# Two feed-forward projections by seven block products each instead of eight

## The chip, the cores and the metric

The kernel runs on one core of a Trainium2 chip: TensorE (PE in the rows, PEld its weight loads), VectorE (DVE), ScalarE (ACT), GpSimd (POOL), and SyncE (SP), whose queue issues nearly all DMA transfers. The metric is the device time of one execution in microseconds (us), the median of several runs.

## The reference, cut to what matters

One layer of a decoder works on 1032 tokens, 1024 of a prompt and 8 of a sample, with 1024 channels in float32:

```python
def layer_forward(h, p_i, ...):
    u = rmsnorm(h, lw['norm_mix'])
    proj = u @ lw['w_in']
    ...
    h = h + jnp.concatenate([y_a, y_b, y_c], axis=-1) @ lw['w_out']
    z = jnp.square(jax.nn.relu(rmsnorm(h, lw['norm_ffn']) @ lw['w_up']))
    h = h + z @ lw['w_down']
    gate = jax.nn.sigmoid(rmsnorm(h, lw['norm_ple']) @ lw['w_ple_gate'])
    h = h + gate * (p_i @ lw['w_ple_proj'])
```

`w_up` is 1024 by 4096, `w_down` 4096 by 1024, the gate's weights 1024 by 1024, and the embedding's projection 256 by 1024. A final norm over `h` gives the output.

## The kernel before, in words

Channels lie on the 128 partitions, tokens along the free axis: a tile is [128, 1032]. The residual `h` is eight such tiles, which stay in SBUF from the output projection to the end. A product keeps float32 accuracy by splitting both operands into a high and a low part of the fast matmul type: three matmuls (weight high times activation high, high times low, low times high; L256, L257, L258) stand for one. A product of 1032 tokens is made as three chunks of 344 columns, each in a PSUM bank of its own.

Weights come in blocks of 512 KB ([128, 1024]). A ring of three raw tiles takes them (L196, SP's queue); ACT writes the high part (L205), DVE or POOL the low part, raw minus high (L206). The ring for high and low parts has three places too.

The stages are: the input projection and, beside it, the three mixers; the output projection, which adds into `h`; the feed-forward; the gate with the embedding; the final norm. The feed-forward goes in eight blocks of 512 hidden channels. Per block four weight blocks go up (8 contraction tiles x 3 x 3 chunks = 72 matmuls each) and four go down (72 each): 64 x 72 = 4608 matmuls. The next block's first up product is put before a block's down products. The eviction of an up chunk is `evac_up`: DVE rectifies and scales by the norm's factor (L1155), ACT squares (L1156), DVE writes the high part (L1157) and the low part (L1158) into tiles which the down products read at once. The eviction of a down chunk is one addition into `h` from PSUM (L1092). POOL has nothing to do here.

In the gate stage the 1024 by 1024 gate product runs over two spans of 384 tokens first, for all eight output tiles, and then over the last 264 tokens. Per output tile the embedding's product (12 matmuls a tile in the first pass, 6 in the second) follows it in a second bank, and `evac_gate` takes both banks. The final norm's factor is turned and spread over the partitions by small matmuls (L307) which stand amid the 264-wide part; POOL multiplies 768 columns a tile by it (L1269), and the last 264 are finished at the end (L1282 to L1293).

The order on each engine is not written by hand: the program's builder orders instructions by a list schedule with costs and priorities of its own, and each engine works its list in that order. Transfers are issued on eight lanes, so that a ninth waits for the oldest of the eight.

Of the kernel before, what the change touches and what calls it, by code (L numbers as in the profile page):

```python
# [8 lines left out]
F32 = mybir.dt.float32  # L9
# [13 lines left out]
LEVELS = (1, 2, 4, 8, 16, 32, 64)  # L23

VEC = {}          # name -> (first column, columns) in the table of per-channel vectors
# [8 lines left out]
TAB = {}          # name -> (first column, columns) in the table of constants  # L34
# [18 lines left out]
class Builder:  # L53
# [7 lines left out]
    def pools(self):  # L61
# [5 lines left out]
        pp = ctx.enter_context(tc.tile_pool(name="psum", bufs=1, space=bass.MemoryType.PSUM))  # L67
# [9 lines left out]
        self.bank = [pp.tile([128, 512], F32, name=f"ps{i}") for i in range(8)]  # L77
        self.mains, self.P = deque(self.bank[:4]), deque(self.bank[4:])

# [50 lines left out]
    def step(self):  # L130
        """One stage of the next chain that can go on; False if none can."""
# [52 lines left out]
    def weights(self, aps):  # L184
        """The blocks to come, each with the engine for its low part."""
# [4 lines left out]
    def entry(self, i):  # L190
        """Block i's tiles: high part, low part, raw."""
# [38 lines left out]
    def tile_mm_k(self, i, kof, xs, evac, free=None):  # L230
        """As tile_mm with the K tiles outside, for operands that come or go one by one."""
# [43 lines left out]
    def rsqrt(self, out, v, t):  # L275
        """out = v ** -0.5: a guess from the exponent, a Newton step of tuned constants (to 7e-4), a cubic step."""
# [1154 lines left out]
```

## Time and profile before

The time is 1633.91 us, the median of 3 runs (1630.21 to 1635.50). The profiled execution has a span of 1635.9 us.

| | PE | DVE | ACT | POOL |
|---|---|---|---|---|
| busy, us | 1586.9 | 978.9 | 436.6 | 285.6 |
| share of the span | 97% | 60% | 27% | 17% |
| instructions | 10251 | 1761 | 558 | 267 |

A row of groups reads: line, engine, operation, output and inputs by their names in the program, shapes and types, count, then busy time in us, mean in ns, and idle time of the engine just before with what ended it. A row of a window lists the stretch, then for PE, PE's weight load, DVE, ACT and POOL the busy time and the number of instructions, then the clock that TensorE was granted (1.00 is full), the share of the DMA engines and GB/s. A row of a timeline begins with the start and the duration in us.

### The profile page before, as it was taken

The page shows a single profiled execution, that of the slowest core. Times are in us where ns is not written, and L with a number is a line of the kernel's source. Part 1 is how long each engine was busy: PE and PEld are TensorE (multiplying, and loading weights), DVE is VectorE, ACT ScalarE, POOL GpSimd, SP SyncE. Part 2 cuts the span into 40 slices and gives each one's busy share as a digit, 9 for nine tenths or more (in the row PEclk, how much of TensorE's full clock was granted, in tenths as well). Part 3 has the DMA queues.
Part 4 walks back from the last instruction along what each step waited for, and adds up shares of the span by engine and source line. Part 5 has one row for each costly group of instructions (what it writes and reads, how often), then busy time and mean ns, then how long its engine had stood idle before and what let it go on. Part 6 is the DMA issues. An engine that isn't in the chain of part 4 may idle for free.

```text
span 1635.9 us, 24167 instructions
## 1 busy us (share of the span) xinstructions
PE 1586.9 (97%) x10251; PEld 1561.6 (95%) x10251; DVE 978.9 (60%) x1761; ACT 436.6 (27%) x558; POOL 285.6 (17%) x267
## 2 busy tenths in 40 slices
PE   7999999999989898999999999999999999999995
PEld 7999999998989898999999999999999999999995
DVE  7787877975887977456534444343444434466556
ACT  5212111124464372133211111120211111134442
POOL 5333233224255442000000000000000000012204
PEclk9999999999999998999999999999999999999998
DMA  5011111111211234241111111111111111121123
GB/s 205 28 34 47 44 47 34 40 53 59 67 54 52 94 119 139 91 146 49 39 52 51 41 52 39 52 49 42 52 39 52 52 40 52 39 78 65 52 65 117
DMA packets 34364, 103.21 MB, mean 63 GB/s; under 512 B 5584, under 2 KB 8272, under 8 KB 34256
## 3 DMA queue, kind: packets, MB, share of 16 engines
q1 hardware_dynamic: 34256, 101.67, 19.4%
q8 instruction: 80, 1.31, 0.3%
q14 instruction: 28, 0.23, 0.0%
HBM read 87.39 MB, written 14.26 MB: 62 GB/s over the span
## 4 chain that ended last, share of the span: by engine, by line
PE 70%; DVE 10%; ACT 2%; issue 2%; POOL 2%; DMA 1%; SPq 0%; POOLq 0%; ACTq 0%; DVEq 0%
PE ps L257 21%; PE ps L256 21%; PE ps L258 21%; DVE g L336 2%; PE ps L414 1%; POOL f L1269 1%; PE ps L240 1%; DVE g L420 1%; PE ps L746 1%; DVE g L334 1%; PE ps L852 1%; DMA o_sss<-f 1%; DVE g L866 0%; DVE f L816 0%; PE ps L307 0%
## 5 line engine op out<-in xcount | busy, mean ns | idle before, releaser
L257 PE MATMUL ps<-r,wh 128*128 128x344 f32 (+2 forms) x2700 | 877.8, 325 | 0.0
L256 PE MATMUL ps<-r,wh 128*128 128x344 f32 (+2 forms) x2700 | 875.4, 324 | 0.0
L258 PE MATMUL ps<-r,wl 128*128 128x344 f32 (+2 forms) x2700 | 871.5, 323 | 0.0
L257 PEld LDWEIGHTS ps<-r,wh 128*128 128x128 f32 x2700 | 510.1, 189 | 3.5 <-issue 2.2
L256 PEld LDWEIGHTS ps<-r,wh 128*128 128x128 f32 x2700 | 510.6, 189 | 2.7 <-issue 1.7
L258 PEld LDWEIGHTS ps<-r,wl 128*128 128x128 f32 x2700 | 510.2, 189 | 3.1 <-issue 1.7
L205 ACT ACTIVATE wh<-raw 128x1024 fp32r<-128x1024 f32 x123 | 130.3, 1059 | 625.4 <-PE ps L257 461.4
L1092 DVE TENSOR_TENSOR f<-f,ps 128x344 f32<-128x344 f32 x240 | 122.2, 511 | 232.4 <-PE ps L258 229.1
L329 POOL TENSOR_TENSOR r<-f,r 128x1032 fp32r<-128x1032 f32 x2 | 4.8, 2408 | 790.8 <-ACT r L328 790.8
L1155 DVE SCALAR_TENSOR_TENSOR f<-ps,f 128x344 f32<-128x344 f32 x96 | 49.5, 516 | 139.2 <-PE ps L258 137.7
L206 POOL TENSOR_TENSOR wl<-raw,wh 128x1024 fp32r<-128x1024 f32 x39 | 96.4, 2473 | 197.2 <-ACT wh L205 197.0
L206 DVE TENSOR_TENSOR wl<-raw,wh 128x1024 fp32r<-128x1024 f32 x84 | 105.8, 1260 | 35.0 <-ACT wh L205 34.7
L1156 ACT ACTIVATE f<-f 128x344 f32<-128x344 f32 x96 | 46.6, 486 | 188.8 <-DVE f L1155 188.7
L1157 DVE CAST r<-f 128x344 fp32r<-128x344 f32 x96 | 36.3, 378 | 34.8 <-ACT f L1156 34.7
L1158 DVE TENSOR_TENSOR r<-f,r 128x344 fp32r<-128x344 f32 x96 | 49.5, 517 | 2.9
L420 DVE COPY_PREDICATED g<-tab,ps 128x512 f32<-128x512 int32 x42 | 37.3, 892 | 14.8 <-PE ps L414 14.2
L414 PE MATMUL ps<-f,g 128*128 128x128 f32 x336 | 45.0, 278 | 0.8 <-DVE g L430 0.8
L414 PEld LDWEIGHTS ps<-f,g 128*128 128x128 f32 x336 | 42.6, 191 | 1.9 <-DVE g L430 1.7
L1005 DVE TENSOR_TENSOR g<-ps,f 128x344 f32<-128x344 f32 x63 | 32.0, 509 | 12.8 <-PE ps L258 9.4
L323 ACT ACTIVATE r<-f,vec 128x1032 fp32r<-128x1032 f32 (+1 forms) x26 | 28.1, 1085 | 35.5 <-DVE f L1092 33.0
L324 DVE SCALAR_TENSOR_TENSOR r<-f,vec,r 128x1032 fp32r<-128x1032 f32 (+1 forms) x26 | 33.7, 1298 | 4.3 <-ACT r L323 4.1
L683 POOL TENSOR_TENSOR r<-tab,dtl 128x256 fp32r<-128x256 f32 x32 | 25.9, 813 | 57.7 <-PE ps L736 56.5
(428 smaller groups left out, 1625.8 us busy)
## 6 DMA issues: line engine op xcount, KB each, us to landing
raw<-wu SPq DMA_DIRECT2D x32, 512.0 KB, 3.6
raw<-wd SPq DMA_DIRECT2D x32, 512.0 KB, 3.5
raw<-win SPq DMA_DIRECT2D x31, 512.0 KB, 3.6
raw<-wg SPq DMA_DIRECT2D x16, 512.0 KB, 3.6
f<-x SPq DMA_DIRECT2D x15, 516.0 KB, 5.7
raw<-wo SPq DMA_DIRECT2D x12, 512.0 KB, 3.7
o_y<-f SPq DMA_DIRECT2D x8, 384.0 KB, 2.3
g<-ya SPq DMA_DIRECT2D x4, 516.0 KB, 4.7
```

Source lines behind the costliest of these rows:

```text
L205: self.nc.scalar.activation(wh, raw, AF.Copy)
L206: self.wq[i][1].tensor_tensor(wl, raw, wh.bitcast(F32), op=OP.subtract)
L256: nc.tensor.matmul(ps, a, xh[:, cs], start=(k == 0), stop=False)
L257: nc.tensor.matmul(ps, a, xl[:, cs], start=False, stop=False)
L258: nc.tensor.matmul(ps, b, xh[:, cs], start=False, stop=(k == last))
L414: nc.tensor.matmul(ps[:, w * 128:(w + 1) * 128].rearrange("p (h k m) -> p h k m", h=2, m=m), d["k"][:, w * 128:(w + 1) * 128], qv[:, :, w ...
L420: V.copy_predicated(d["att"][:, :1024].rearrange("p (a k two m) -> p a k two m", a=8, two=2, m=m)[:, :, :, 1, :], mask.rearrange("p (k m) ...
L1092: V.tensor_tensor(h[m][:, cs], h[m][:, cs], ps, op=OP.add)
L1155: V.scalar_tensor_tensor(tz[:, cs], ps, 0.0, norm.rB[:, cs], op0=OP.max, op1=OP.mult)
L1156: A.activation(tz[:, cs], tz[:, cs], AF.Square)
L1157: V.tensor_copy(hi[:, cs], tz[:, cs])
L1158: V.tensor_tensor(lo[:, cs], tz[:, cs], hi[:, cs].bitcast(F32), op=OP.subtract)
```

## The change

Both feed-forward products are cut into halves of output channels, of contraction and of tokens (516 each), and made by the Winograd form of Strassen's scheme: seven products of half size instead of eight, for which sums of quarters are needed on both sides and sums of products behind.

*Weights.* They are laid out by quarters; four quarter sums per unit are made on POOL (L1529 to L1532), and seven pieces are split into high and low (L347 on ACT, L348 on DVE). This is done by `Feed`, which also issues the transfers (L1525).

*Activations going in.* `PairNorm` replaces the norm that came before the feed-forward: as each output tile of `h` is done, it is scaled (ACT), squared (ACT), summed (POOL or DVE), and stored to DRAM; for each pair of tiles four sums of 516 columns are made (POOL; DVE for the last pair), and seven results are split into high and low. 28 tiles hold these operands.

*Up.* A unit is 256 hidden channels; 16 units of 7 products, each 4 contraction tiles x 3 x 2 chunks of 258 columns = 24 matmuls: 2688. Two chunks lie in two banks, a pair; four pairs take the seven products in the order 0, 2, 1, 0, 2, 1, 3, where products 3, 4 and 5 go on adding to the pair of 0, 1 and 2 (product 3 adds to product 0, 4 to 1, 5 to 2). So each of these three waits until the pair it goes on with has been read out: product 3 for L1262, product 4 for L1264, product 5 for L1266. The four quarters of the hidden activations are squared, and four more are made from them by POOL (L1273 to L1287), one of which is overwritten on the way. The seven operands for the down product are split (L1243 on ACT, L1244 on DVE) into a staging tile, high and low side by side, and stored to DRAM (L1245). Units 14 and 15 stay in SBUF.

*Down.* 32 units: eight blocks of contraction (512 channels, two up units) by four pairs of output tiles, each unit 7 products of 12 matmuls: 2688. `h` is loaded again from DRAM (L1372), the products are read out by DVE and ACT, and sums of results on POOL finish three of the four quarters. The operands of a block are loaded again while the block before is at work: 14 tiles of 516 KB at its end (L1418), the first 14 in the first unit (L1415).

*Embedding.* Its product (192 matmuls of 258 columns) now stands between up and down; its result goes to DRAM (L1359) and is loaded again for the gate stage (L1167), where `evac_gate` reads it from SBUF instead of from PSUM. The gate stage has the gate product alone.

PSUM is cut anew twice, into four pairs for the feed-forward and back into eight banks. In the changed program L275 to L277 are the three matmuls of `mm_chunk`, L316 and L326 the two small products of the final norm, and L224/L225 the weights' high and low parts outside the feed-forward.

```diff
-        norm = self.trunk_norm(h, "norm_ffn")
+        norm = PairNorm(self, h, "norm_ffn")
+        up = Feed(self, [io["wu"][i] for i in range(16)], 512, [self.raw[k] for k in (2, 0, 1)],
+                  [self.wr[k] for k in (2, 0, 1)])
...
-        for i, (kind, b, m) in enumerate(order):
-            if kind == "u":
-                self.tile_mm(i, 0, hg, evac_up(b, m))
...
-                    self.tile_mm(i, n * 4, z4, add_h(mm, norm2.add if b == 7 else None), ahead=(n == 0))
...
+        norm.rest()
+        up.advance(0)
+        self.pair = self.psum("pp", 4)
+        zd = self.ffn_up(norm, up)
+        h = self.ffn_down(norm, up, zd)
...
-                for s, ps, pe in zip(spans, pg, pp):
-                    self.mm_chunk(pe, *wp[m // 4], (m % 4) * 2, p, s)
-                    evac_gate(m, s, ps, pe)
+                for s, ps in zip(spans, pg):
+                    evac_gate(m, s, ps, pe[m][:, s])
...
+    def product(self, n, w, q, ks, last):
+        wh, wl, off = w
+        acc = self.pair[ACC[n]]
+        for k in ks:
+            a, b = (t[:, off + k * 128:off + (k + 1) * 128] for t in (wh, wl))
+            for i, (l, o) in enumerate(((a, 0), (a, HF), (b, 0))):
+                for c in range(2):
+                    self.nc.tensor.matmul(acc[:, c * 512:c * 512 + CQ], l, q[k][n][:, o + c * CQ:o + (c + 1) * CQ],
...
+        def spill(n, t):
...
+            A.activation(hi.bitcast(F32R), t, AF.Copy)
+            V.tensor_tensor(lo.bitcast(F32R), t, hi, op=OP.subtract)
+            nc.sync.dma_start(zd[-1][n], st)
...
+        def act(t, r, src=None):
+            V.scalar_tensor_tensor(two(t), two(t) if src is None else src, 0.0, two(r), op0=OP.max, op1=OP.mult)
+            A.activation(t, t, AF.Square)
+
+        def evac(n):
+            ps = self.acc(n)
+            if n == 0:
+                A.activation(two(t1), ps, AF.Copy)
+            elif n == 1:
+                A.activation(two(t5), ps, AF.Copy)
+            elif n == 2:
+                V.tensor_tensor(two(t2), ps, two(t1), op=OP.subtract)
+            elif n == 3:
+                act(a0, rb[0], ps)
+                spill(0, a0)
+            elif n == 4:
+                V.tensor_tensor(two(a1), ps, two(t2), op=OP.subtract)
+                act(a1, rb[1])
+                G.tensor_tensor(v1, a0, a1, op=OP.subtract)
+                spill(1, v1)
+            elif n == 5:
+                V.tensor_tensor(two(t3), ps, two(t1), op=OP.subtract)
+                G.tensor_tensor(b1, t3, t5, op=OP.subtract)
+                act(b1, rb[1])
+                G.tensor_tensor(t2_, b1, v1, op=OP.add)
+                spill(4, b1)
+                G.tensor_tensor(v3, a1, b1, op=OP.subtract)
+                spill(2, t2_)
+                spill(5, v3)
+            else:
+                V.tensor_tensor(two(b0), ps, two(t3), op=OP.add)
+                act(b0, rb[0])
+                G.tensor_tensor(v4, b0, t2_, op=OP.subtract)
+                spill(3, b0)
+                spill(6, v4)
...
+                    if j == 3 and b < 6:
+                        for k in range(2):
+                            nc.sync.dma_start(qs[k][n].bitcast(F32), zd[2 * b + 2 + k][n])
...
+                if i == self.groups - 1:
+                    a11, s1, s2, a12, s4, a21, a22 = (self.piece(u, n) for n in range(7))
+                    G.tensor_tensor(s1, a21, a22, op=OP.add)
+                    G.tensor_tensor(s2, s1, a11, op=OP.add)
+                    G.tensor_tensor(s4, s2, a12, op=OP.add)
+                    G.tensor_tensor(a21, a21, a11, op=OP.add)
```

In a row of the order stands the line, the operation, output and inputs by tile (`f` a float32 tile, `r` a tile of split operands, `wh` and `wl` weights' high and low parts, `raw` weights as loaded, `ps` and `pp` PSUM banks and pairs) and the shape. In the kernel before, DVE in the middle of an up product of the feed-forward works through these rows:

```order
L1155 SCALAR_TENSOR_TENSOR f4_96<-ps3_111,f8_100 128x344 [waits PE_49]
L206 TENSOR_TENSOR wl0_87<-raw0_90,wh0_86 128x1024 [waits DMAHW2_49,Activation_49]
L1157 CAST r2_6_5572<-f4_96 128x344 [waits Activation_49]
L1158 TENSOR_TENSOR r2_7_5573<-f4_96,r2_6_5572 128x344 [waits DVE_49]
L1155 SCALAR_TENSOR_TENSOR f7_99<-ps0_108,f8_100 128x344 [waits PE_49]
```

In the change, DVE in a steady up unit, around the reads of products 2 (L1266), 3 (L1256 from `pp0`) and 4 (L1271):

```order
L1244 TENSOR_TENSOR f1_90<-f8_97,f1_90 128x516 [waits DMAHW6_49,Activation_49]
L1244 TENSOR_TENSOR f4_93<-f3_92,f4_93 128x516 [waits DMAHW0_49,Activation_49]
L1266 TENSOR_TENSOR f0_89<-pp1_6209,f0_89 128x516 [waits PE_49]
L1244 TENSOR_TENSOR f11_100<-f8_97,f11_100 128x516 [waits DMAHW2_49,Activation_49]
L1256 SCALAR_TENSOR_TENSOR f5_94<-pp0_6208,f6_95 128x516 [waits PE_49]
L348 TENSOR_TENSOR wl2_5564<-raw1_88,wh2_5563 128x1024 [waits Activation_49]
L1244 TENSOR_TENSOR f1_90<-f5_94,f1_90 128x516 [waits DMAHW3_49,DVE_49,Activation_49]
L1271 TENSOR_TENSOR f5_94<-pp2_6210,f0_89 128x516 [waits PE_49]
L1256 SCALAR_TENSOR_TENSOR f5_94<-f5_94,f6_95 128x516 [waits DVE_49]
L1276 TENSOR_TENSOR f2_91<-pp1_6209,f0_89 128x516 [waits PE_49]
```

Where evictions stood with one low part of a weight among them, low parts of the unit before (L1244), which wait for ACT and for the store that last used their staging tile (the DMAHW semaphores), now stand before and between the reads of PSUM. POOL, which had no row in the feed-forward, has nine in each up unit of the change:

```order
L1273 TENSOR_TENSOR f10_99<-f5_94 128x516 [waits Activation_49]
L1277 TENSOR_TENSOR f3_92<-f2_91 128x516 [waits DVE_49]
L1279 TENSOR_TENSOR f10_99<-f3_92,f10_99 128x516 [waits Activation_49]
L1281 TENSOR_TENSOR f8_97<-f5_94,f3_92 128x516
L1529 TENSOR_TENSOR raw0_87<-raw2_5565,f7_96 128x512 [waits DMAHW2_49,DMAHW0_49]
L1287 TENSOR_TENSOR f8_97<-f3_92,f10_99 128x516 [waits Activation_49,Pool_49]
L1530 TENSOR_TENSOR raw1_88<-raw0_87 128x512 [waits DMAHW1_49,Pool_49]
L1532 TENSOR_TENSOR raw2_5565<-raw2_5565,raw0_87 128x512
L1531 TENSOR_TENSOR raw2_5565<-raw1_88 128x512 [waits DMAHW6_49,Pool_49]
```

All nine have two operands in SBUF (a name that stands once covers two halves of one tile), and the sums of weights stand among those of results. SP at the end of a down block, where SP before had a weight block now and then:

```order
L1525 DMA raw1_88<-wd 128x256 [waits DMAHW6_49]
L1418 DMA r2_8_5574<-z4_0_7166 128x1032 [waits DMAHW7_49,PE_49]
L1418 DMA r3_69<-z5_0_7397 128x1032 [waits DMAHW0_49,PE_49]
L1418 DMA r2_9_5575<-z4_1_7167 128x1032 [waits DMAHW1_49,PE_49]
L1418 DMA r4_70<-z5_1_7398 128x1032 [waits DMAHW2_49,PE_49]
...
L1418 DMA r0_66<-z4_4_7170 128x1032 [waits DMAHW7_49,PE_49]
L1525 DMA raw0_87<-wd 128x256 [waits DMAHW0_49,DVE_49]
L1525 DMA raw0_87<-wd 128x256 [waits DMAHW1_49,Pool_49]
L1418 DMA r7_73<-z5_4_7401 128x1032 [waits DMAHW2_49,PE_49]
L1525 DMA raw1_88<-wd 128x256 [waits DMAHW3_49,DVE_49]
L1418 DMA r1_67<-z4_5_7171 128x1032 [waits DMAHW4_49,PE_49]
```

The reloads wait for PE to be done with the tiles of the block before (PE_49), and pieces of weights (L1525) stand behind them in the one queue.

More of the change, by code (lines that the diff above doesn't have):

```diff
@@ L1209, in build @@
                 wh, wl = self.block(i)
-                pg, pp = ([self.main_bank()[:, :s.stop - s.start] for s in spans] for _ in range(2))
+                pg = [self.main_bank()[:, :s.stop - s.start] for s in spans]
                 for s, ps in zip(spans, pg):
@@ new lines, in embed_part, with embed @@
+    def embed_part(self, n, raw, hi, lo):
+        w = T if n < 2 else 1024
+        self.nc.sync.dma_start(raw[:, :w], self.io["p" if n < 2 else "wp"][n % 2])
+        self.split(raw[:, :w], hi[:, :w], lo[:, :w])
+    def embed(self, q, out):
+        self.pe, nc = [], self.nc
+        for m in range(8):
+            t = out[m % 2]
+            d = self.dp.tile([128, T], F32, name=f"pe{m}")
+            for s in range(2):
+                acc = self.pair[(0, 2, 1, 3)[(2 * m + s) % 4]]
+                for k in range(2):
+                    xh, xl = q[0][k], q[1][k]
+                    wh, wl = (q[i][2 + m // 4][:, (m % 4 * 2 + k) * 128:(m % 4 * 2 + k + 1) * 128] for i in (0, 1))
+                    for i, (l, r) in enumerate(((wh, xh), (wh, xl), (wl, xh))):
+                        for c in range(2):
+                            o = s * HF + c * CQ
+                            nc.tensor.matmul(acc[:, c * 512:c * 512 + CQ], l, r[:, o:o + CQ],
+                                             start=(k == 0 and i == 0), stop=(k == 1 and i == 2))
+                nc.scalar.activation(t[:, s * HF:(s + 1) * HF].rearrange("p (c t) -> p c t", c=2),
+                                     acc.rearrange("p (c t) -> p c t", c=2)[:, :, :CQ], AF.Copy)
+            nc.sync.dma_start(d, t)
+            self.pe.append(d)
@@ new lines, with __init__, add, pair @@
+class PairNorm:
+    def __init__(self, b, h, gname):
+        self.b, self.h, self.gname = b, h, gname
+        self.u, self.q, self.hd, self.later = [], [], [], []
+        self.ssq = self.rB = None
+    def add(self, m):
+        b, nc = self.b, self.b.nc
+        A, G, V = nc.scalar, nc.gpsimd, nc.vector
+        hm = self.h[m]
+        u = b.get_main()
+        A.activation(u, hm, AF.Copy, scale=b.col(self.gname, m))
+        self.u.append(u)
+        if m == 0:
+            self.ssq = b.get_main()
+            A.activation(self.ssq, hm, AF.Square)
+        else:
+            t = b.get_main()
+            A.activation(t, hm, AF.Square)
+            (G if m < 6 else V).tensor_tensor(self.ssq, self.ssq, t, op=OP.add)
+            b.put(t)
+        self.hd.append(b.dp.tile([128, T], F32, name=f"h{m}"))
+        nc.sync.dma_start(self.hd[m], hm)
+        b.put(hm)
+        if m % 2:
+            self.pair(m // 2)
+    def pair(self, k):
+        b, nc = self.b, self.b.nc
+        E = nc.vector if k == 3 else nc.gpsimd
+        ua, ub = self.u[2 * k:2 * k + 2]
+        v = b.get_main()
+        b11, b12, b21, b22, v1, t2 = (t[:, o:o + HF] for t in (ua, ub, v) for o in (0, HF))
+        v3 = b12
+        self.q.append([None] * 7)
+        def split(n, t):
+            def go():
+                q = self.q[k][n] = b.R.popleft()
+                b.split(t, q[:, :HF], q[:, HF:])
+            if b.R and not self.later:
+                go()
+            else:
+                self.later.append(go)
+        split(0, b11)
+        E.tensor_tensor(v1, b11, b12, op=OP.subtract)
+        split(1, v1)
+        E.tensor_tensor(t2, b22, v1, op=OP.add)
+        split(2, t2)
+        split(3, b21)
+        split(4, b22)
+        E.tensor_tensor(v3, b12, b22, op=OP.subtract)
+        split(5, v3)
+        def last():
+            E.tensor_tensor(b21, b21, t2, op=OP.subtract)
+            split(6, b21)
+        if self.later:
+            self.later.append(last)
+        else:
+            last()
+        self.later.append(lambda: b.put(ua, ub, v)) if self.later else b.put(ua, ub, v)
+    def rest(self):
+        todo, self.later = self.later, []
+        for f in todo:
+            f()
+        assert not self.later
+        self.rB = self.b.get_main()
```

253 lines of the change are left out of this document (196 added, 57 removed).

## The prediction

> **What bounds the kernel now.** I read first the totals, the slices and the shares of the chain on the profile's page, then the windows of the feed-forward, then single rows for prices.
>
> ```profile
> span 1635.9 us, 24167 instructions
> PE 1586.9 (97%) x10251; PEld 1561.6 (95%) x10251; DVE 978.9 (60%) x1761; ACT 436.6 (27%) x558; POOL 285.6 (17%) x267
> DVE  7787877975887977456534444343444434466556
> POOL 5333233224255442000000000000000000012204
> PE 70%; DVE 10%; ACT 2%; issue 2%; POOL 2%; DMA 1%; SPq 0%; POOLq 0%; ACTq 0%; DVEq 0%
> ```
>
> PE is busy for 97% of the span and carries 70% of the chain. From slice 17 (about 700 us) to slice 37, DVE is about 40% busy and POOL idle: that is the feed-forward. There every matmul counts, and DVE, ACT, POOL and the DMA queues are covered. The windows give the pace (columns: busy time and instructions of PE, weight load, DVE, ACT, POOL; then clock, DMA share, GB/s):
>
> ```profile
> 0.00:50.00 50.00, 40.05 (x227) 37.22 (x228) 35.56 (x66) 25.03 (x32) 23.10 (x22) 0.97 0.53 179
> 1000.00:1100.00 100.00, 100.00 (x636) 100.00 (x636) 41.24 (x76) 15.64 (x23) 0.00 (x0) 1.00 0.16 48
> 1561.00:1576.00 15.00, 15.00 (x87) 15.00 (x87) 8.79 (x15) 5.74 (x9) 0.00 (x0) 1.00 0.16 47
> 1591.60:1596.60 5.00, 5.00 (x42) 5.00 (x43) 3.97 (x15) 2.26 (x4) 0.00 (x0) 1.00 0.39 102
> ```
>
> 100 us hold 636 matmuls of 344 columns: 157.2 ns each. The third row is the gate stage with 384 columns: 15/87 = 172 to 175 ns. The fourth has 264 columns: 5.00/42 = 119 ns. The time goes with the columns, down to 264. The feed-forward's 4608 matmuls (64 weight blocks of 72) take 4608 x 157.2 = **724.5 us** of the span.
>
> **The change: matmuls.** 48 units (16 up of 7 x 24, 32 down of 7 x 12) issue 5376 matmuls of 258 columns. Of that width there is no row. Bounds: the 264 row less 6 columns at its own slope gives 116, its first starts at most 122; I take 119 ns. An up unit is then 168 x 0.119 = 20.0 us, a down unit 10.0 us, each half 320 us, together 640: 85 us less, where PE never waits. The question is whether the other engines keep that pace, since each unit brings much new work for them.
>
> **The change: an up unit.** Prices, DVE and ACT first, then POOL, then the rows where the two meet (in timeline rows: start, duration; in the others, count, busy, mean ns, or minimum/median/maximum):
>
> ```profile
> L818 DVE TENSOR_TENSOR f<-f 128x512 f32<-128x512 f32 x8 | 5.5, 686 | 1.4 <-POOL f L815 1.3
> L694 DVE TENSOR_TENSOR g<-ps,dt 128x512 f32<-128x512 f32 x6 | 4.0, 685 | 1.2 <-PE ps L692 1.0
> L763 DVE SCALAR_TENSOR_TENSOR g<-g,vec,ps 128x512 f32<-128x512 f32 x8 | 5.9, 740 | 1.2 <-PE ps L761 1.2
> L441 ACT ACTIVATE g<-ps 128x512 f32<-128x512 f32 x5 | 3.0, 598 | 29.0 <-PE ps L440 29.0
> L206 DVE TENSOR_TENSOR wl<-raw,wh x84: 1211/1226/2852, 589.8 to 1609.0; 128x1024 fp32r<-128x1024 f32 x84
> L1269 POOL TENSOR_TENSOR f<-f,f x8: 1845/2044/2825, 1600.2 to 1615.5; 128x768 f32<-128x768 f32 x8
> L1289 POOL TENSOR_TENSOR raw<-f,f 128x264 f32<-128x264 f32 x3 | 2.1, 740 | 11.8 <-ACT f L1282 11.8
> L329 POOL TENSOR_TENSOR r<-f,r 128x1032 fp32r<-128x1032 f32 x2 | 4.8, 2408 | 790.8 <-ACT r L328 790.8
> L205 ACT ACTIVATE wh<-raw 128x1024 fp32r<-128x1024 f32 x123 | 130.3, 1059 | 625.4 <-PE ps L257 461.4
> ```
>
> POOL: 768 columns take 1.845 us and 264 take 0.74, so 2.19 ns a column, and 512 or 516 take 1.28 us. A unit has nine (five of L1273 to L1287, four weight sums of L1529 to L1532): 11.5 us. DVE, two operands in SBUF: 7 low parts of 516 (L1244, 0.69 each), 3 rectifications (L1256, about 0.7), the weights' low parts (L348, three of 1024 at 1.23, one of 512 at 0.69): 14 operations, 11.3 us. DVE, one operand in PSUM: 5 (L1266, L1256, L1271, L1276, L1285) at 0.69: 3.5 us. ACT has 7 high parts, 4 squares, 2 copies and the weights' high parts (1.06 for 1024 columns, 3.8 in all): 13 x 0.62 + 3.8 = 12 us. So DVE 14.8, ACT 12, POOL 11.5 of PE's 20.0: apart, all fit. But before the change POOL stood still in this stage; the end of the program shows DVE beside a busy POOL:
>
> ```profile
> 1600.15 6.63 POOL L1269 TENSOR_TENSOR f<-f,f 128x768 f32<-128x768 f32 x3 [45.68 <-ACT f L318]
> 1598.82 0.43 DVE L1198 TENSOR_TENSOR f<-f,f 128x264 f32<-128x264 f32 x1
> 1600.42 1.87 DVE L1203 TENSOR_TENSOR f<-f,f 128x264 f32<-128x264 f32 x1 [1.17 <-ACT f L1202]
> 1602.21 0.42 DVE L1195 TENSOR_TENSOR f<-ps,f 128x264 f32<-128x264 f32 x1
> 1602.56 2.53 DVE L206 TENSOR_TENSOR wl<-raw,wh 128x1024 fp32r<-128x1024 f32 x1
> 1605.01 0.42 DVE L1197 TENSOR_TENSOR f<-f,ps 128x264 f32<-128x264 f32 x1
> 1605.46 1.62 DVE L1198 TENSOR_TENSOR f<-f,f 128x264 f32<-128x264 f32 x1
> ```
>
> A DVE operation with both operands in SBUF takes 0.43 us alone and 1.62 to 1.87 while POOL works; one that reads PSUM takes 0.42 either way. POOL is stretched too: 1.845 to 2.04 (median) beside a 0.43 us operation, to 2.83 beside one of 1.23 us. So they take turns, and a turn costs POOL 0.20 or 0.98, DVE's own duration less about 0.24; at 516 columns about 0.46. A turn of nine is then 1.28 + 0.46 = 1.74, and nine of them, 15.7 us, let nine of DVE's 14 through (9 x 0.69 = 6.2 of its 11.3 us). The other 5.1 us and the five PSUM reads (3.2 us at a pitch of 0.63) come on top: 24.0, less two PSUM reads which fall under a POOL turn: **22.8 us a unit**, and not 20.0. DVE sets the pace, and PE waits: L1266, which empties product 2's bank for product 5, stands behind low parts of the unit before. Four units are lighter (0 starts without spills in its way, 14 and 15 store nothing): 21 each. Up: 12 x 22.8 + 4 x 21 = **358 us**.
>
> In sentences of their own: the Trainium skill, "SBUF — State Buffer", "Who interferes with whom", says that VectorE and GpSimd share one port pair as an exclusive lock, that a VectorE instruction with two SBUF inputs contends with one of GpSimd that reads SBUF, and that the later fully blocks. The rows agree on who is hit (0.43 against 1.62 to 1.87; 0.42 with PSUM), but not on the whole duration: POOL's row grew by 0.20 for an operation of 0.43.
>
> Stores: 98 tiles of 516 KB go out and come back. With 1 MB of weights an up unit moves 4.6 MB in 22.8 us, 203 GB/s; the first window moved 179 GB/s at a share of 0.53, so the engines of the DMA queues hold it. Three staging tiles rotate, a store has about 9 us until its tile is wanted. I cost the stores at nothing; their cover is that slack.
>
> **A down unit.** POOL 4 sums of 256 (0.72 by the slope) and 3 of 516: 6.7 us. DVE: 6 reads of PSUM (3.8) and the weights' low parts (1.23, and 0.92 for 768 columns): 6.0 us. Should every POOL sum make DVE wait in full for a turn it would be 12.7, but only the two low parts, of 13 operations on the two engines, have both operands in SBUF: with a wait of 1.28 before each, 8.5 of 10.0. PE stays the bound: 320 us. SP now carries the reloads too; at the end of each of six blocks 14 tiles are asked for at once, in front of and between weight pieces (L1525):
>
> ```profile
> raw<-wd SPq DMA_DIRECT2D x32, 512.0 KB, 3.5
> raw_e<-win SPq DMA_DIRECT2D x1, 512.0 KB, 9.9
> ```
>
> Alone 512 KB land in 3.5 us, in the crowd of the first loads in 9.9; weights are fetched about two units (20 us) early. So mostly covered; for seven bursts I add 5 us (bounds 0 and 45, below): **325 us**.
>
> **The way in and the gate.** As the last output tiles come, POOL gets 5 sums of 1032 (2.4 each) and 12 of 516, and the first weights' 4: 32 us, where PE has some 45 us of products; 28 splits on DVE run against it, the last eight after tiles come free. I add **5 us** (0 to 12). The embedding's 192 matmuls before the down half cost 192 x 0.119 = 22.8 us. The gate stage loses 96 of 384 columns (16.8 us) and 48 of 264. The latter gains nothing, because the end hangs on the final factor:
>
> ```profile
> 1584.46 0.29 PE L256 MATMUL ps<-r,wh 128*128 128x264 f32 x1
> 1597.89 1.50 PE L307 MATMUL ps<-ident,nscr 128*128 128x128 f32 x12
> PE ps L307 <- DVE nscr L287: 1.8, 1, 1.8
> ```
>
> L307 comes 13.4 us after the 264 part's start, POOL's L1269 2.3 us later, and 35.8 us after that all is over. In the new order 137 such matmuls precede it instead of 99: 38 x 0.119 = 4.5 us later, less up to 1.8 which PE then waited. Net 22.8 - 16.8 + 3.9 = **9.9 us** (0 to 15).
>
> **Sum** against the profiled 1635.9: 1635.9 - 724.5 + 5 + 358 + 325 + 9.9 = 1609.3. The profiled execution lies 0.1% above the median of the runs, 1633.9; so 1607.
>
> **Rivals.** (1) *No price for turns*: the queues slide past each other, up runs at PE's 20.0: 320 instead of 358, 1607 - 38 = 1569. For it: DVE has 14.8 us of work, and its low parts have a whole unit's slack; against it, the 1.62 to 1.87 rows. (2) *DVE and POOL exclude each other wholly*: 11.5 + 11.3 = 22.8 for the two-operand work, and all five PSUM reads behind it, 3.5: 26.3 us a unit, 16 x 3.5 = 56 more: 1663, slower. The deciding point is 1607 + 16 x (u - 22.8) = 1634: u = 24.5 us a unit. For it: the 2.53 and 2.85 us rows of 1024 columns; against it, POOL's stretch of only 0.20. By the sentence of the Trainium skill on blocking ("SBUF — State Buffer", as above) this would be the outcome. (3) *Reload bursts starve the down half*: the program lets eight transfers be outstanding; 14 tiles at 9.9 us for eight take 17 us, and the weight piece behind it lands up to 6.4 us late, seven times: +45, 1652; slower from 3.9 us a burst on. For it: the order below L1418's rows; against it, the pieces asked for two units early. (4) *The change does less than it says*: it doesn't; the new order holds 2688 + 2688 + 192 matmuls of 258.
>
> **Chances.** The forecast (DVE sets the pace in up, PE in down) 0.57, no price 0.20, full exclusion 0.14, bursts 0.09. The forecast's own range is 1588 to 1630: 116 to 122 ns in the down half gives 8 us either way, the unit's turns 21.5 to 24, the way in 0 to 12, the gate 0 to 15. 8 of 10 takes in most of the no-price case and leaves out the far half of the slow ones: 1566 to 1648. What a measurement can tell from no change is about 0.3%, 1629 to 1639. Faster: 0.20 and nearly all of 0.57: 0.75. Same: the forecast's upper edge, 0.06. Slower: 0.14 + 0.09 less their mild ends, and a little of the forecast: 0.19.
>
> **What would show it.** Right: in windows of the up half PE has about 147 matmuls of 258 columns per 20 us instead of 168, and its waits at the products name DVE's L1266, L1271 and L1276; L1244 means over 1.0 us instead of 0.69, POOL's 516 sums about 1.7. The down half stands at 100% PE, 420 matmuls in 50 us. Wrong: L1244 at 0.7 us and PE full in up (rival 1); units of 25 us and more (rival 2); PE waiting in down for splits of weights whose L1525 pieces landed late (rival 3); a store's tile as the releaser of L1243 would mean the DMA's slack was none; or the first split products waiting more than 12 us at the way in.

## The result

The change makes the kernel slower: 1658.99 us, the median of 4 runs (1657.78 to 1660.30), against 1634.04 us before. The ratio is 1.0156, with a 95% interval of 1.0135 to 1.0176. The forecast was 1607 in a range of 1566 to 1648, so the time lies 11 us outside it and on the other side of the time before.

From the page of the changed kernel (totals, then the busy tenths in slices of 41.5 us each):

```profile
span 1658.2 us, 27796 instructions
PE 1538.6 (93%) x11067; PEld 1504.4 (91%) x11067; DVE 1260.5 (76%) x1798; ACT 607.1 (37%) x810; POOL 825.7 (50%) x650
DVE  7777787876886885559699999989356676679576
POOL 5423232224355441037477666766367677777214
```

PE's busy time fell by 48 us only, DVE's rose by 282 and POOL's by 540. In slices 20 to 27 (the first is 0), the up half, DVE stands at 9, once at 8. The chain of the page can't be set against the 70% of before: here it goes back only to 1099.5 us, and its shares add up to 34% of the span.

The stages can be cut at PE's instructions: start of the second half of the output projection, first and last feed-forward matmul, end. Here are the windows of the kernel before (second half of the output projection, which the table calls the way in, feed-forward, gate and end), and then of the change (the same second half, up, embedding, down, gate and end). The columns are those of the earlier windows.

```profile
720.50:765.70 45.20, 45.20 (x289) 45.20 (x288) 31.52 (x41) 18.71 (x18) 0.00 (x0) 1.00 0.15 48
765.70:1496.60 730.90, 730.90 (x4649) 730.90 (x4648) 323.58 (x567) 132.50 (x183) 9.64 (x4) 1.00 0.16 49
1496.60:1635.90 139.30, 122.85 (x792) 122.45 (x791) 82.71 (x138) 51.95 (x83) 33.91 (x17) 0.94 0.23 76
```

```profile
716.40:778.10 61.70, 47.92 (x290) 46.72 (x288) 49.16 (x52) 32.03 (x42) 39.38 (x21) 0.96 0.26 95
778.10:1148.70 370.60, 343.53 (x2725) 340.62 (x2726) 335.53 (x314) 182.84 (x277) 242.85 (x139) 0.96 0.53 196
1148.70:1184.10 35.40, 26.21 (x193) 24.76 (x193) 17.79 (x18) 14.93 (x27) 16.36 (x13) 0.95 0.86 309
1184.10:1526.20 342.10, 331.16 (x2691) 327.60 (x2690) 230.55 (x261) 92.09 (x110) 245.66 (x212) 0.99 0.55 199
1526.20:1658.20 132.00, 106.24 (x649) 104.44 (x647) 87.28 (x142) 52.91 (x84) 39.82 (x20) 0.88 0.28 98
```

The feed-forward before took 730.9 us, and the forecast takes 724.5 of them out. The 6.4 that it leaves belong to 36 small matmuls of the norm's factor, about 4 us, and to a matmul of 344 columns that takes 157.7 ns from start to start and not 157.2. In the change the 36 stand in the first two up units, so the table puts the 6.4 there.

| stage | forecast, us | measured, us | difference |
|---|---|---|---|
| up to the second half of the output projection | 720.5 | 716.4 | -4.1 |
| way in (45.2 before) | 50.2 | 61.7 | +11.5 |
| up, 16 units (358), with the 6.4 left over | 364.4 | 370.6 | +6.2 |
| embedding | 22.8 | 35.4 | +12.6 |
| down, 32 units | 325 | 342.1 | +17.1 |
| gate and end (139.3 before) | 126.4 | 132.0 | +5.6 |
| sum | 1609.3 | 1658.2 | +48.9 |

No stage missed by more than 17.1 us; five of them missed in the same direction. What PE waited for, the longest and those of the gate's start (engine, line, whom for; us in all, times, longest):

```profile
PE pp L1218 <- DVE f L1266: 24.3, 11, 3.5
PE ps L275 <- DVE f L1111: 7.5, 3, 4.1
PE pp L1355 <- ACT f L1357: 7.4, 5, 3.3
PE pp L1218 <- DVE f L1111: 6.3, 1, 6.3
PE pp L1218 <- ACT wh L347: 5.3, 3, 2.5
PE pp L1218 <- DVE f L1384: 3.3, 1, 3.3
PE pe L275 <- ACT r L342: 3.2, 1, 3.2
PE pe L276 <- DVE r L343: 2.3, 1, 2.3
```

The first row is the forecast's wait in the up half. The second and fourth are the way in, the third the embedding, the next two the down half, and the last two the gate's start.

The waits are not all that PE loses, because its clock falls behind some of them. These are PE's first products of the up half, after a wait of 6.26 us, and a group of four matmuls 5 us later:

```profile
778.06 1.20 PE L1218 MATMUL pp<-r,wh 128*128 128x258 f32 x4 [6.26 <-DVE f L1111]
779.49 1.06 PE L1218 MATMUL pp<-r,wh 128*128 128x258 f32 x4
783.22 0.64 PE L1218 MATMUL pp<-r,wh 128*128 128x258 f32 x4
```

And in the up half, behind a wait of 2.62 us:

```profile
936.87 1.23 PE L1218 MATMUL pp<-r,wh 128*128 128x258 f32 x4 [2.62 <-DVE f L1266]
938.32 1.06 PE L1218 MATMUL pp<-r,wh 128*128 128x258 f32 x4
940.52 0.64 PE L1218 MATMUL pp<-r,wh 128*128 128x258 f32 x4
```

The clock's record shows stretches at half rate, 3.4 us long or a multiple of that. Behind the middle of the program (from 700 us on) they cost 39 us of clock in the change, and 9 before, all of the latter at the very end, where PE has little to do. 9 of the 39 lie there too. In the up half they are 14 us, and the 12 behind its first unit fall on time in which DVE sets the pace (from 828 to 1104 us DVE waits for PE once, 0.5 us). The others, in the way in, at the first up products, in the embedding, the down half and at the gate's start, lie on PE's path, but for some 2 us in which PE waits anyway.

### The profile page after: what moved, and what is told of

The parts are those of the page before. It is cut to its first block, busy times and chain, and to the rows that moved or that the text cites. A ratio compares the mean times of both kernels' runs of the same rounds, so it can differ in the third digit from the quotient of the medians.

```text
span 1658.2 us, 27796 instructions
## 1 busy us (share of the span) xinstructions
PE 1538.6 (93%) x11067; PEld 1504.4 (91%) x11067; DVE 1260.5 (76%) x1798; ACT 607.1 (37%) x810; POOL 825.7 (50%) x650
## 5 line engine op out<-in xcount | busy, mean ns | idle before, releaser
L1218 PE MATMUL pp<-r,wh 128*128 128x258 f32 x3584 | 589.8, 288 | 43.6 <-DVE f L1266 24.3
L1218 PEld LDWEIGHTS pp<-r,wh 128*128 128x128 f32 x3584 | 503.9, 194 | 49.5 <-DVE f L1266 26.9
L1218 PE MATMUL pp<-r,wl 128*128 128x258 f32 x1792 | 362.9, 286 | 0.7 <-DVE wl L348 0.5
L275 PE MATMUL ps<-r,wh 128*128 128x344 f32 x972 | 323.2, 333 | 7.5 <-DVE f L1111 7.5
L276 PE MATMUL ps<-r,wh 128*128 128x344 f32 x972 | 323.6, 333 | 0.0
L277 PE MATMUL ps<-r,wl 128*128 128x344 f32 x972 | 319.9, 329 | 0.0
L1218 PEld LDWEIGHTS pp<-r,wl 128*128 128x128 f32 x1792 | 282.1, 193 | 1.5 <-DVE wl L348 1.5
L275 PEld LDWEIGHTS ps<-r,wh 128*128 128x128 f32 x972 | 185.9, 191 | 11.2 <-issue 6.1
L276 PEld LDWEIGHTS ps<-r,wh 128*128 128x128 f32 x972 | 185.7, 191 | 3.3 <-issue 1.9
L277 PEld LDWEIGHTS ps<-r,wl 128*128 128x128 f32 x972 | 185.5, 191 | 2.9 <-issue 1.5
L348 DVE TENSOR_TENSOR wl<-raw,wh 128x1024 fp32r<-128x1024 f32 x102 | 151.5, 1493 | 30.8 <-ACT wh L347 30.6
L225 POOL TENSOR_TENSOR wl<-raw,wh 128x1024 fp32r<-128x1024 f32 x39 | 98.3, 2520 | 153.6 <-ACT wh L224 153.5
L347 ACT ACTIVATE wh<-raw 128x1024 fp32r<-128x1024 f32 x102 | 96.4, 946 | 172.0 <-POOL raw L1530 108.6
L1244 DVE TENSOR_TENSOR f<-f,f 128x516 fp32r<-128x516 f32 x98 | 142.5, 1476 | 8.1 <-ACT f L1243 7.9
L224 ACT ACTIVATE wh<-raw 128x1024 fp32r<-128x1024 f32 x59 | 62.3, 1056 | 220.6 <-PE ps L276 127.6
L1243 ACT ACTIVATE f<-f 128x516 fp32r<-128x516 f32 x98 | 62.0, 635 | 91.4 <-DMA z<-f 65.4
L348 DVE TENSOR_TENSOR r<-f,r 128x516 fp32r<-128x516 f32 (+2 forms) x53 | 66.1, 1270 | 8.5 <-ACT r L347 8.2
L275 PE MATMUL pe<-r,wh 128*128 128x384 f32 (+1 forms) x192 | 62.7, 327 | 3.2 <-ACT r L342 3.2
L276 PE MATMUL pe<-r,wh 128*128 128x384 f32 (+1 forms) x192 | 63.2, 329 | 2.3 <-DVE r L343 2.3
```

The source lines that it names most:

```text
L224: self.nc.scalar.activation(wh, raw, AF.Copy)
L225: self.wq[i][1].tensor_tensor(wl, raw, wh.bitcast(F32), op=OP.subtract)
L275: nc.tensor.matmul(ps, a, xh[:, cs], start=(k == 0), stop=False)
L276: nc.tensor.matmul(ps, a, xl[:, cs], start=False, stop=False)
L277: nc.tensor.matmul(ps, b, xh[:, cs], start=False, stop=(k == last))
L347: nc.scalar.activation(hi, x, AF.Copy)
```

## The experiments

Theories: **turns** (DVE operations with two operands in SBUF and POOL's take turns, so DVE sets the pace of the up half), and for each other stage a theory of its own, stated with the run. Times by stage are cut as above.

**The sums of the up half on DVE.** The five sums of results and, from unit 1 on, the four of weights:

```diff
-                G.tensor_tensor(v1, a0, a1, op=OP.subtract)
+                V.tensor_tensor(v1, a0, a1, op=OP.subtract)
...
                 if i == self.groups - 1:
+                    G = nc.vector if self.kw == 512 and u > 0 else nc.gpsimd
                     a11, s1, s2, a12, s4, a21, a22 = (self.piece(u, n) for n in range(7))
```

> In the up half (units 1 to 15) all nine sums of a unit move from POOL to DVE: five of results, four of weights; POOL is idle there. Theory (turns at the operands in SBUF): DVE's low part L1244 falls from a mean of 1.48 us to 0.70; DVE has 13.5 us of its own and 5.5 us of sums, 19.0 a unit, under PE's 20.0; a unit takes 20.0 to 20.6 us in place of 23.1, the up half about 325 in place of 371, the whole about 1613 us (1605 to 1625) against 1659. Rival (DVE is slow for its volume and for the stores that ACT's L1243 waits for, 65 us in sum): L1244 stays near 1.4 us and 5.5 us more work make 28.6 us a unit, about 1745 us.

Measured: 1619.07 us, ratio to before 0.9903 (0.9872 to 0.9934). The up half fell from 370.6 to 331.0, and units 2 to 14 all took 20.2 or 20.3 us. The group of low parts, in the change and then in this run, and a window of 23.1 us of this run, about a unit of the change, with two of the sums that moved:

```profile
L1244 DVE TENSOR_TENSOR f<-f,f 128x516 fp32r<-128x516 f32 x98 | 142.5, 1476 | 8.1 <-ACT f L1243 7.9
```

```profile
L1244 DVE TENSOR_TENSOR f<-f,f 128x516 fp32r<-128x516 f32 x98 | 67.2, 690 | 5.1 <-ACT f L1243 5.1
900.00:923.10 23.10, 23.10 (x194) 23.10 (x193) 21.38 (x33) 12.21 (x20) 0.00 (x0) 1.00 0.63 232
...
935.32 0.69 DVE L1279 TENSOR_TENSOR f<-f,f 128x516 f32<-128x516 f32 x1
935.93 0.69 DVE L1281 TENSOR_TENSOR f<-f,f 128x516 f32<-128x516 f32 x1
```

DVE has nine operations more in a unit and needs less time for all of them (18.8 us of a unit of 20.2, from 850 to 1090 us, against 21.7 of 23.1 from 828 to 1104 us in the change), since none stands behind POOL. PE is full, at full clock. The rival (volume and stores) is out: it forecast 1745. ACT's waits for the stores were long in the change (59 us at L1243 in those 276 us) and nearly went with the turns (3.2 us in 240), so they came of the pace and did not make it. In the change the turn had the forecast price: POOL's sums of 512 and 516 that met DVE, and DVE's operations in turn with them, took this (start, duration; POOL first):

```profile
952.19 1.47 POOL L1529 TENSOR_TENSOR f<-raw,raw 128x512 f32<-128x512 f32 x1 [0.23 <-DMA raw<-wu]
953.62 1.75 POOL L1287 TENSOR_TENSOR f<-f,f 128x516 f32<-128x516 f32 x1
955.33 1.76 POOL L1530 TENSOR_TENSOR raw<-f 128x512 f32<-128x512 f32 x1
```

```profile
952.44 1.77 DVE L348 TENSOR_TENSOR wl<-f,wh 128x512 fp32r<-128x512 f32 x1
954.13 5.21 DVE L1244 TENSOR_TENSOR f<-f,f 128x516 fp32r<-128x516 f32 x3
959.27 0.68 DVE L1266 TENSOR_TENSOR f<-pp,f 128x516 f32<-128x516 f32 x1
```

Three low parts in 5.21 us are 1.74 each, the forecast's 1.28 + 0.46, and the read of PSUM that PE waits for, L1266, comes behind them at 0.68. Where the Trainium skill ("SBUF — State Buffer", "SBUF: two separate sides") has the later of two such operations block fully, a turn would take 1.28 + 0.69 = 1.97, an estimate from these rows; the rows show 1.74.

**Five tiles for the embedding's result.**

```diff
-        self.embed(norm.q, fx)
+        self.embed(norm.q, [*fx, *stage])
...
-            t = out[m % 2]
+            t = out[m % len(out)]
```

> The embedding's result goes out through five tiles instead of two, nothing else. Theory (PE waits for ACT, ACT for a tile whose store stands in the crowd of reloads): the waits of 9.2 us at the embedding and 1.7 us of low clock behind them vanish, the embedding takes 24 to 26 us instead of 35.4, the whole about 1649 us. Rival (the DMA engines are full from 1160 to 1180 us, whoever waits): the waits move to the first down products, the whole stays at 1659.

Measured: 1655.82 us, ratio 1.0136 (1.0112 to 1.0160). The embedding's stage took 27.0 us in place of 35.4, its wait for L1357 1.0 us in place of 7.4. The theory holds for the stage. In the change ACT's copies, two at a time, had stood behind the stores like this:

```profile
1175.38 1.09 ACT L1357 ACTIVATE f<-pp 128x516 f32<-128x516 f32 x2 [5.36 <-DMA pe<-f]
```

Of the 8.4 us gained there the profiled span keeps 6.3 (1651.9 for 1658.2) and the median 3.2: PE's waits for L347 rose from 5.3 to 8.9 us in sum, and the down half and the gate took 0.6 and 1.2 us more. That is not the rival, which put the waits at the first down products: these ran without one, and the longer waits stand behind the later bursts.

**Reloads spread over three units.** In place of two tiles a product in the last unit of a block:

```diff
+                    if j < 3 and b < 7:
+                        nx = q[:2] if b % 2 == 0 else q[2:]
+                        for i in range((j * 7 + n) * 2 // 3, (j * 7 + n + 1) * 2 // 3):
+                            nc.sync.dma_start(nx[i % 2][i // 2].bitcast(F32), zd[2 * b + i % 2][i // 2])
```

> The 14 reloads of a block are issued two in three products over the first three units of the block before, instead of two a product in its last unit (the first block: over three units instead of one). Theory (weight pieces land late behind a burst): the waits at the ends of blocks (2.5, 2.1 and 0.8 us, their low clock, some of 0.3 us) vanish, 8 to 10 us, the whole about 1650. Rival (POOL's chain of weight sums is late by itself): PE waits for L347 and L348 as before, 1659.

Measured: 1661.49 us, ratio 1.0163 (1.0142 to 1.0185); the down half 341.9 us. No gain, but no answer either: the transfers did not spread. SP's rows of this run at the end of a block (start, time from the first issue to the last of the group, count):

```profile
1278.02 20.28 SPq L1523 DMA_DIRECT2D raw<-wd  x11
1298.63 0.33 SPq L1416 DMA_DIRECT2D r<-z  x1
1300.31 0.33 SPq L1523 DMA_DIRECT2D raw<-wd  x1
1300.73 5.86 SPq L1416 DMA_DIRECT2D r<-z  x9
```

SP works its list in order. A weight piece whose tile is not yet free holds it up, the reloads gather behind, and nine go out at once, with the next pieces behind them.

**The sums of the way in on DVE.** Those of pairs, of squares, and of unit 0's weights:

```diff
-        E = nc.vector if k == 3 else nc.gpsimd
+        E = nc.vector
...
-            (G if m < 6 else V).tensor_tensor(self.ssq, self.ssq, t, op=OP.add)
+            V.tensor_tensor(self.ssq, self.ssq, t, op=OP.add)
```

> Before the up half all sums go to DVE: those of pairs, of squares, and of unit 0's weights; the up units stay as they are. Theory (turns): splits there fall from 1.75 to 2.1 us to 0.7, DVE has about 50 us of work for PE's 45, so PE waits for about 5 us instead of 16: the whole about 1649 us. Rival (DVE's volume decides there): 15 us more work on DVE make the way in longer by up to 15: 1665 to 1674.

Measured: 1651.88 us, ratio 1.0108 (1.0089 to 1.0128); the way in 50.6 us in place of 61.7. The theory holds: 11 us, with more work on DVE, whose splits of 516 columns all take 0.69 us or less. What is left is a wait of 5.0 us for L1111, the last evictions of the output projection.

**The down half without reloads.** The two places that load operands again (L1415, L1418) are left out, so the result is not the layer's and only the times count.

> The operands of the down half are not loaded again from DRAM (98 transfers of 516 KB left out; the down products use what lies in the tiles, so the result is not the layer's). Everything else stays. Theory A (pieces of weights stand behind the reloads in SP's queue): all waits of the down half up to unit 26 (2.6, 2.2, 0.9 us and six of 0.2 to 0.4) vanish, the embedding's waits too, since its stores lose the crowd (35 to about 24 us): the down half about 335 us instead of 342, the whole about 1640. Theory B (POOL's chain of sums is late by itself): the same waits stay in the down half, 342 us.

Measured: 1644.73 us in one run; the down half 326.4 us in place of 342.1. All waits up to unit 26 are gone, and unit 30 takes 12.4 us in place of 16.7. The down half lost about 16 us to the reloads, as theory A says. Whether by SP's order or by their load this run alone can't tell, since it takes both away. Theory A was wrong on the embedding, which stayed at 35.2: its crowd is not made by these transfers. In the change, the burst and what POOL waited for behind it read so (POOL's sums of weights stand until their pieces have landed):

```profile
1299.13 5.25 SPq L1418 DMA_DIRECT2D r<-z  x9
1305.35 3.29 SPq L1525 DMA_DIRECT2D raw<-wd  x3
1309.59 4.92 SPq L1418 DMA_DIRECT2D r<-z  x4
1316.30 0.73 POOL L1529 TENSOR_TENSOR raw<-raw 128x256 f32<-128x256 f32 x1 [3.17 <-DMA raw<-wd]
```

**The last block's norm work later.** At products 2 and 5 of the next unit instead of at the unit's end:

```diff
+                    if b == 7 and j and n in (2, 5):
+                        norm2.add(2 * j - 2 + (n == 5))
```

> In the last down block the norm's work on a pair of output tiles (two low parts and two sums of squares on DVE) is asked for later: at products 2 and 5 of the next unit, and after the last unit for the last pair. Theory (reads of PSUM stand behind the norm's work in DVE's queue): units 29 and 30 go from 11.9 and 16.7 us to about 10.5, the waits at the gate's start grow by 1 to 4 us: 1653 to 1656 us. Rival (DVE has more work than PE in this block, wherever it stands): what the units lose is waited for at the gate: 1659.

Measured: 1661.83 us, ratio 1.0174 (1.0157 to 1.0190). Unit 30 took 15.7 us in place of 16.7, unit 29 as before. The theory falls. With the run without reloads it is seen why: late weights were part of unit 30's loss (12.4 us there, in place of 16.7), not only the order on DVE.

**The gate's first two tiles together**, contraction tile by contraction tile:

```diff
+                        for k in range(8):
+                            for (wh, wl), pg in zip(ws, pgs):
+                                for s, ps in zip(spans, pg):
...
+                            if k % 3 == 2:
+                                self.tick()
```

> The gate stage's first two output tiles are made together, contraction tile by contraction tile, so that the last two, which DVE still splits, are wanted after 12.6 us instead of 3.2. Theory: the waits of 3.2 and 2.3 us and 6.8 us of low clock behind them vanish, and the end comes 8 to 12 us earlier: 1647 to 1651. Rival (the end hangs on the last norm's factor and on DVE's work in the gate stage): PE waits less at the start and more later, 1659.

Measured: 1660.77 us, ratio 1.0166 (1.0146 to 1.0186); the gate and end 132.9 us. The waits changed their names: the matmuls of the norm's factor (L316) now stood among the products and waited for the same late sum, and low parts on POOL came late. Rows of this run:

```profile
PE pe L316 <- DVE f L1659: 3.6, 1, 3.6
PE pe L1205 <- POOL wl L225: 2.2, 1, 2.2
```

A later run (below) puts the factor behind these products and the gate's low parts on DVE.

**Together.** The sums of the way in and the up half on DVE, five tiles, the later norm work, the gate's first two tiles:

> All together: the sums of the way in and of the up half on DVE, five tiles for the embedding's result, the later norm work, the gate's first two tiles together. If each edit is worth what its stage showed alone (up 40, way in 11, embedding 8) and unit 0 loses 5 less to a late start, 1659 - 64 = 1595; with the gate's 8 to 12 and 3 from the last block 1580 to 1585. If the stages share one cover (an engine that is late hands its lateness on), about 1600 to 1610.

Measured: 1598.06 us, ratio 0.9787 (0.9765 to 0.9808). Way in 50.6, up 331.0, embedding 21.7, down 342.8, gate and end 133.7: the gains add up, and the two edits that gave nothing alone give nothing here. (12 of the embedding's matmuls now stand behind the first of the down half, 1.4 us of that stage.)

**Reloads from another queue.** The sums of the way in and of the up half on DVE, five tiles, and the spread reloads issued by ACT, and in a second run by POOL; this second run also has the gate's two tiles with the factor behind them:

```diff
-                            nc.sync.dma_start(nx[i % 2][i // 2].bitcast(F32), zd[2 * b + i % 2][i // 2])
+                            nc.scalar.dma_start(nx[i % 2][i // 2].bitcast(F32), zd[2 * b + i % 2][i // 2])
```

(`nc.gpsimd` in the second.)

> All sums of the way in and of the up half on DVE and five tiles for the embedding's result, as in the combination (1598), without its two edits at the end of the down half; and the reloads are spread over the first three units of the block before and issued from ACT's queue, where no weight piece stands behind them. Theory A (weights stand behind reloads that SP issues): the down half goes from 342.8 to 327 to 331, the whole to 1582 to 1587. Rival (ACT, which now waits for free lanes of the queue, is late with its reads of PSUM and with high parts): the down half stays at 340 or more, 1598 to 1610.

> The same with the reloads issued from POOL's queue, and at the gate the first two output tiles together with the norm's factor asked for behind them, and all low parts of the gate's weights on DVE. Theory A: the down half 327 to 332; the gate's start without the waits (3.6 and 2.2 us) and the 6.8 us of low clock which the first try left, 125 in place of 133: 1575 to 1580. Rivals: POOL's sums come later for the issues on its queue, and the down half stays at 340; the gate stage ends no earlier since DVE's work there decides: 1598.

Measured: 1636.10 us with ACT, ratio 1.0010 (0.9996 to 1.0023), and 1625.60 us with POOL, ratio 0.9938 (0.9919 to 0.9957). In both the down half took 379 us. What PE waited for, ACT's run first:

```profile
PE pp L1218 <- ACT f L1382: 30.4, 10, 5.9
```

```profile
PE pp L1234 <- DVE f L1413: 13.2, 9, 4.1
PE pp L1234 <- DVE wl L348: 11.7, 5, 3.2
```

The forecast of 327 to 332 fails, and the rivals came true. ACT's run does take away the wait for the weights' high parts (L347: 6.6 us in the combination, none here), but in the order the engine that issues waits for lanes or tiles at its issues, and its own work stands behind (at 1216.74 us ACT had been idle for 11.4 us until a reload landed): PE then waits for ACT's copies of product 0 (L1382) in the one run, for what needs POOL's sums in the other (L1413 is the read of product 6 into a quarter that POOL adds to). The queue was moved and late work came with it, so these two runs do not settle whether weights stood behind SP's reloads. The gate's part was right: gate and end 124.9 us in place of 133.7. Its edit beside the first try:

```diff
-                            if k % 3 == 2:
-                                self.tick()
+                        self.tick()
...
-                    self.weights([(io["wg"][m], e) for e in (G, V) for m in range(8)])
+                    self.weights([(io["wg"][m], e) for e in (V, V) for m in range(8)])
```

**A deeper ring for the down half's weights.** Two tiles more to land in, up to unit 27, so that each piece is asked for about a unit earlier:

```diff
-        feed = Feed(self, [io["wd"][i % 32] for i in range(28, 60)], 256, raws, wr)
+        extra, more = [self.get_main() for _ in range(2)], []
+        feed = Feed(self, [io["wd"][i % 32] for i in range(28, 56)], 256, raws + extra, wr)
```

> The changed kernel with two more tiles in the ring in which the down half's weights land (five groups of pieces instead of three, up to unit 27), so that a piece is asked for one unit (10 us) earlier; reloads, queues and sums stay. Theory A (pieces land up to 3 us too late behind the reloads): the waits at units 10, 13, 18, 21, 25, 26 vanish, the down half goes from 342 to 330 to 334, the whole to 1647 to 1651. Rival (it is the reloads' own load on the DMA engines, or SP's order, whatever the lead): waits as before, 1659.

Measured: 1645.50 us, ratio 1.0071 (1.0054 to 1.0087); the down half 329.3 us. All units but the last two take 10.2 to 10.8 us. The rival falls: the reloads and their bursts are still there, and the pieces only have to be asked for before them. So 13 of the 17 us by which the down half missed were pieces of weights asked for too late.

**The best version.** The sums on DVE, five tiles, the deeper ring, and the gate's two tiles with the factor behind:

> All sums of the way in and of the up half on DVE, five tiles for the embedding's result, the deeper ring of the down half, and at the gate the first two tiles together, the norm's factor behind them, the low parts on DVE. Stage by stage: 718 to the way in, 50.6, 330.3, 21.7, 330 to 334, 125: 1576 to 1580 us, if theory A holds; 1588 if the down half stays at 342.

Measured: **1574.07 us** (1573.37 to 1575.28), ratio 0.9634 (0.9620 to 0.9648): 60 us faster than the kernel before, 85 faster than the change. Its page:

```profile
span 1572.4 us, 27709 instructions
PE 1508.9 (96%) x11067; PEld 1482.4 (94%) x11067; DVE 1206.7 (77%) x1967; ACT 602.7 (38%) x810; POOL 534.3 (34%) x481
DVE  7787887976978778556989999999566666669776
POOL 5333242323354543100000000001478888877004
```

Way in 50.6, up 331.1, embedding 20.2, down 332.7, gate and end 120.4. The embedding has no wait left; 24 of its matmuls, 2.9 us, stand in the down half's first unit, so the two stages are 23.1 and 329.8 by their own work. What the version still loses: 5 us at the up half's start for L1111, 6 us in unit 0 (26.2 for 20.2), and 4 to 5 us in the down half's last two. Most of unit 0's loss can be read from its rows, though no run tried it: 30 of the norm's 36 small matmuls stand in it, about 3 us, and the clock stays at half until 772.7 us, which costs 2.3.

## Why the prediction was wrong

**What bounds: right. The matmuls: nearly.** A matmul of 258 columns takes 120 ns where PE waits for nothing (168 in an up unit of 20.2 us), not 119: a down unit is 10.1 us, which makes 3.5 us in the half. The prediction divided windows by all the matmuls that touch them; from start to start those of 264 columns before took 122 ns and not 119.

**The up unit: right in its mechanism, and nearly in its size.** Twelve middle units took 23.1 us on average (276.7 us; single ones 20.2 to 27), against 22.8. Not all of it is turns: in these units DVE waits for ACT for 1.3 us a unit, which the sum did not have. One sign of being wrong came true as well, since the stores' tiles released L1243 for 65 us in all; the run with the sums on DVE shows that this was no cause. The turn's price, 1.74 us, was read off the end of the kernel before, and the run with the sums on DVE shows that this price, 40 us in the half, is what held DVE. The step that failed here is "four units are lighter, 21 each": units 0, 1, 14 and 15 took 25.2, 23.4, 25.1 and 20.2, 10 us more in sum. In the first two stand the 36 small matmuls of the norm (most of the 6.4 us of the table) and 2.4 us of low clock. Unit 14 stores nothing, but by the order DVE still has low parts of unit 13 in it.

**The way in: the term was mis-sized, 16.5 us for 5** (against 45.2 before). It counted POOL's 32 us against PE's 45 and found room. It did not apply to this stage the price that it had just worked out for the next: there DVE has 28 splits; 21 of them stand before the first up product, and 14 of these took 1.2 to 2.9 us beside POOL's sums, where one alone takes 0.7. The run with these sums on DVE gives 11.1 of the 16.5 back.

**The embedding: the step that failed is 192 x 0.119 with no wait at all.** The term priced matmuls and not what empties their banks. The stage took 12.6 us more. Two tiles for eight results, whose stores stand in SP's queue among loads of `h` and operands, are 8.4 of them: three tiles more bring these back. In the best version, where the half before ends in time, all of it is gone.

**The down half: the right place, mis-sized.** Rival 3 named the burst, its place and the late pieces, and priced it at 45; the sum took 5. The half took 17.1 us more than the sum had for it. The runs give 13 (deeper ring) to 16 (no reloads) to the late pieces. Its sentence "weights are fetched about two units early" was not enough by little: the waits behind the bursts are 0.8 to 2.5 us long, and one unit more removes them. In the last block units 29 and 30 lost 8 us, 5 of them to late weights by the run without reloads; what the rest is, the norm's work for the gate on DVE or something else, stays open, and the prediction had no term for it.

**The gate and the end: 5.6 us too long, two errors of opposite sign.** The products with 384 columns were priced without a wait. The gate's start has waits of 3.2 and 2.3 us, and low clock costs 5.8 more, 11.3 in all. The first product of 264 columns starts at 1608.8 us and L326 comes 18.0 us later, as the forecast's 13.4 + 4.5 says. But from POOL's multiplication to the end it is 29.1 us and not the 35.8 of before:

```profile
1629.11 15.62 POOL L1463 TENSOR_TENSOR f<-f,f 128x768 f32<-128x768 f32 x8 [41.11 <-ACT f L337]
```

That part is 6.7 us of luck; why it is shorter was not tried. The later run with the gate's first two tiles together and the factor behind them takes the stage to 124.9.

**What was left out of all terms is the clock.** A wait of PE was priced at its own length. Behind some of them PE runs at half clock for 3.4 us or more, which costs half of that once more: about 2 us at the first up unit (24 matmuls from 778.06 to 783.22, where 2.9 would do), 1.7 twice in the down half, 5.8 at the gate's start. The Trainium skill ("TensorE: Matmul & The Clock Gate", The HAM clock gate (the "warmup" mystery)) gives a window of about 3.4 us, idle, before the clock falls, and the steps agree; but here waits of 2.6 us were enough in places (at 936.87 us, and not at 913.75 us after 2.68).

**The rivals.** Full exclusion (1663) came out next to the measured time for the wrong reason: the units took 23.1 and not 26.3. No price (1569, the up half at 320) is nearly what that half does once POOL is out of it: 331. The chances gave 0.23 to the slow side, on mechanisms that would each have to be large; what came were five small losses of one sign.

## What to carry to other kernels

When a change takes work from a full engine and gives the others more, price the sides as carefully as the middle: every stage where the engine was full before has no slack in its books, and each new wait there counts in full, with the slow clock behind it. Two operands in SBUF on DVE beside a busy POOL cost a turn each; work that looks balanced over two engines may be faster on one of them. Moving issues to another engine's queue moves the waiting too; asking earlier (a deeper ring) is what helped.

## What the runs showed of the hardware

A DVE operation of 516 columns with both operands in SBUF and a POOL sum of 516 go as a pair in 1.74 us, less than their 1.28 + 0.69 one behind the other; DVE alone does two in 1.2 (L1279 and L1281 start 0.61 us apart in the run with the sums on DVE). A wait of PE of 2.6 us can halve the clock for 3.4 us (at 936.87 us; at 913.75 us one of 2.68 did not). A reload of 516 KB took 7.5 us to land in the change (median), where a weight block of 512 KB (`raw<-wd`) had taken 3.5 in the kernel before:

```profile
r<-z SPq DMA_DIRECT2D x98, 516.0 KB, 7.5
```
